# One store of the block inverses per half of the rows, and an instruction order from the timeline model, in a hybrid mLSTM and gated-delta-rule block

## The chip, the cores and the metric

The kernel runs on one core of one Trainium2 chip. The metric is the time of one execution on the device in microseconds (us). The changed kernel is compared with the kernel before on the same chip.

The core has five engines that this text names as the profile does: PE (TensorE, matmuls; PEld is its weight load), DVE (VectorE), ACT (ScalarE), POOL (GpSimd) and SP (SyncE). Each works through its own list of instructions strictly in order, and waits at an instruction until what it needs is there. DMAs are issued from the lists of SP, POOL and ACT.

## The reference

One encoder block over 256 tokens of 2048 features, in float32: an adaptive norm, one large input projection, two bidirectional mixers, a gated merge, an output projection, and a SwiGLU FFN.

```python
def gated_delta_chunkwise(q, k, v, beta, g):        # 16 heads of 128, CHUNK = 64
    ...
    a_mat = jnp.eye(CHUNK, dtype=jnp.float32) + (
        betac[..., :, None] * jnp.einsum('nbhid,nbhjd->nbhij', kc, kc) * decay_strict)
    t_mat = lax.linalg.triangular_solve(
        a_mat, jnp.broadcast_to(jnp.eye(CHUNK, dtype=jnp.float32), a_mat.shape),
        left_side=True, lower=True, unit_diagonal=True)
    ...
def mlstm_chunkwise(q, k, v, log_i, log_f):         # 4 heads, dk 256, dv 512
    ...
```

Branch A is the mLSTM, branch B the gated delta rule (GDN). The merge is `g_a*y_a + g_b*y_b`, where y_a and y_b are the branches after a projection each. The inverse `t_mat` is what the change touches.

## The kernel before, in words

All weights are read once from DRAM as f32 and split on the chip into a high part (`wh`, by ACT) and the remainder (`wl`, by DVE, which subtracts `wh` from the raw weights). PE multiplies with wh and wl. A weight tile is loaded by SP into one of three buffers `raw`; wh and wl have three buffers each.

The work comes in jobs. `fjob` (L157 to L163; names `b..` for the GDN's q, k, v and `a..` for those of the mLSTM) makes 128 columns out of two halves; a half is one wh on ACT, one wl on DVE and 24 matmuls of 256 columns, 16 on wh and 8 on wl. `tjob` (L182, L183, L200 to L203; names `z`, `v`, `o`, `ma`, `mb`, `ya`, `yb`, `gt`, `up`, `d`) makes 512 columns; each half has one wh, one wl and 12 matmuls of 512 columns, 8 on wh and 4 on wl. Jobs whose result is wanted only later are used to fill PE's time beside steps that need little PE (`fill` in the code, "fill jobs" below).

The stages in order of time: the first 130 us read the adaptive norm's weights and the first input weights; then to some 965 us the GDN, in four groups g0 to g3 of four heads, with fill jobs; the mLSTM with the output projections of both branches and the merge to about 1360 us; then the FFN to the end.

A group of the GDN has these steps:

- `gdn_phase1` for each head: convolution (`cv`, L298 to L301), norms, the decay-weighted Gram matrices `mi`. The 32x32 blocks on their diagonals go through DRAM (`inst_d`, L604) into the tile `uu` (L607), one block per partition, 64 blocks for the group.
- `gdn_invert`: DVE inverts the 64 blocks of 32x32 at once, from row 30 up to row 0, with one product (`utmp`, L635) and one addition (L641) a row. Rows 16 to 31 are stored to `inv_d` in DRAM after step 16, rows 0 to 15 at the end, by POOL (L627).
- `gdn_blocks`: POOL reads `inv_d` back into `cg` (L654), another layout of the same blocks. It takes the buffer of `uu`. DVE transposes it (L656) and mixes it into `R` (L660, L661); ACT copies it into `X` (L669) and `UL` (L674).
- `gdn_phase2` for each pair of heads: matmuls `p` (L689, L698, L723) on R, X and UL, then the recurrences, and at the end `px` (L772), `obt` (L774) and its store to `ob_d` (L775, issued from ACT).

After the last group the GDN's pools are closed (`sx.close()`), and the tiles of the mLSTM take their place. So POOL's loads for the mLSTM wait for the last uses of the GDN's tiles, the store of the last `obt` among them: `o` (L895, the GDN's result, split into `obh` and `obl`, L899 and L900, which the job `yb` multiplies), and for each head `mkq`, `vt`, `sgo` and `bc` (L904 to L911). `psc` (L924) multiplies mkq; `mdec` (L915 to L918, L933 to L936) is made from bc and psc; `pden` and `ph` use mdec.

The order of the instructions on each engine isn't the order of the code. The framework schedules the traced program on a model of the engines, and emits each engine's list in the order that comes out. Instructions that the code wraps in `order` (L85) keep the program's order among themselves:

```python
def order(ins, yes=True):
    return tc.keep_in_program_order(ins) if yes else ins
```

The model used is set where the context is made (L1361), `tile.TileContext(nc)`.

## Time and profile before

| | |
|---|---|
| median of 3 runs | 2038.97 us (2037.25 to 2042.45) |
| the profiled execution | 2036.88 us, its span 2035.0 us |
| mean granted TensorE clock | 0.987 |
| PE busy | 1956.7 us (96%) |
| DVE, ACT, POOL busy | 1394.1, 1050.0, 106.4 us |
| read from DRAM, written | 467.07 MB, 16.82 MB; 238 GB/s over the span |
| chain that ended last | PE 70%, DMA 11%, DVE 9%, ACT 6% |

The span runs from the first to the last instruction of the profiled execution; 1.88 us lie around it. A row of the timeline has the start, the duration, engine, line, operation, tiles (buffer numbers left out) and, in brackets, the idle time of the engine just before and what ended it. A row of the waits has the total, the number of times and the longest.

### The profile page before, as it was taken

The numbers are of one execution on the slowest core, as the hardware profiler recorded it, in microseconds if no ns is written. First come the engines' busy times: TensorE is split into PE (matmuls) and PEld (weight loads), VectorE is DVE, ScalarE is ACT, GpSimd is POOL, SyncE is SP. The second block draws the span as 40 slices with busy tenths as digits, with TensorE's granted clock in tenths as the row PEclk, the third lists the DMA queues.
The fourth block names the chain that finished last, engine by engine and source line by source line (L and its number), as shares of the span: only waits on it lengthen the run. The fifth ranks groups of instructions, "written<-read, shape, count | busy, mean of one in ns | idle before, by whom it ended". The sixth has DMA issues, their size and how long they took to land.

```text
span 2035.0 us, 27065 instructions
## 1 busy us (share of the span) xinstructions
PE 1956.7 (96%) x10374; PEld 1706.4 (84%) x10374; DVE 1394.1 (69%) x2059; ACT 1050.0 (52%) x1582; POOL 106.4 (5%) x205
## 2 busy tenths in 40 slices
PE   8999999999999899999899999999999999999997
PEld 6777879988888788988878788778888888888886
DVE  5778777777889588855677679866666665555554
ACT  3147547755775577565444444554444444444443
POOL 0002210010101010100200000000000000000000
PEclk9999999999999899999999999999999999999999
DMA  9986664556766465766987669656767666566563
GB/s 399 420 325 222 178 215 153 190 171 220 241 230 197 178 211 212 243 238 240 360 297 264 212 245 390 256 186 249 252 244 262 235 246 212 204 206 204 199 200 142
DMA packets 78962, 485.64 MB, mean 239 GB/s; under 512 B 10585, under 2 KB 15969, under 8 KB 24433
## 3 DMA queue, kind: packets, MB, share of 16 engines
q1 hardware_dynamic: 63360, 450.95, 61.2%
q0 software_dynamic: 8160, 17.88, 3.8%
q10 hardware_dynamic: 7314, 15.10, 2.0%
q8 instruction: 81, 1.33, 0.3%
q14 instruction: 47, 0.39, 0.1%
HBM read 467.07 MB, written 16.82 MB: 238 GB/s over the span
## 4 chain that ended last, share of the span: by engine, by line
PE 70%; DMA 11%; DVE 9%; ACT 6%; issue 2%; POOL 1%; ACTq 0%; SPq 0%; DVEq 0%; POOLq 0%
PE acc_up L200 4%; PE acc_up L203 4%; PE acc_up L201 4%; PE acc_d L201 4%; PE acc_d L200 4%; PE acc_d L203 4%; PE acc_gt L201 4%; PE acc_gt L200 4%; PE acc_gt L203 4%; PE acc_b L161 3%; DMA ra<-ada 3%; DMA ada<-ada 2%; PE acc_o L203 2%; PE acc_o L200 2%; PE acc_o L201 2%
## 5 line engine op out<-in xcount | busy, mean ns | idle before, releaser
L183 DVE TENSOR_TENSOR wl_d<-raw_d,wh_d 128x1024 fp32r<-128x1024 f32 x88 | 107.5, 1225 | 105.4 <-ACT wh_d L182 103.1
L183 DVE TENSOR_TENSOR wl_up<-raw_up,wh_up 128x1024 fp32r<-128x1024 f32 x88 | 107.6, 1225 | 100.4 <-ACT wh_up L182 100.4
L126 DVE SCALAR_TENSOR_TENSOR ada<-ada,crow 128x2048 f32<-128x2048 f32 x64 | 146.6, 2290 | 24.1 <-DMA ada<-ada 24.0
L182 ACT ACTIVATE wh_d<-raw_d 128x1024 fp32r<-128x1024 f32 x88 | 92.9, 1056 | 124.5 <-PE acc_d L201 114.3
L183 DVE TENSOR_TENSOR wl_gt<-raw_gt,wh_gt 128x1024 fp32r<-128x1024 f32 x88 | 107.7, 1224 | 69.9 <-ACT wh_gt L182 68.4
L182 ACT ACTIVATE wh_up<-raw_up 128x1024 fp32r<-128x1024 f32 x88 | 92.9, 1057 | 120.9 <-PE acc_up L201 71.6
L161 PE MATMUL acc_b<-hh,wh_b 128*128 128x256 f32 x576 | 142.0, 288 | 9.6 <-ACT wh_b L157 8.0
L182 ACT ACTIVATE wh_gt<-raw_gt 128x1024 fp32r<-128x1024 f32 x88 | 92.9, 1055 | 108.9 <-PE acc_gt L201 61.3
L161 PE MATMUL acc_b<-hl,wh_b 128*128 128x256 f32 x576 | 139.6, 284 | 0.0
L201 PE MATMUL acc_gt<-wh_gt,hfl 128*128 128x512 f32 x352 | 136.9, 389 | 0.0
L200 PE MATMUL acc_gt<-wh_gt,hfh 128*128 128x512 f32 x352 | 135.6, 385 | 0.0
L200 PE MATMUL acc_up<-wh_up,hfh 128*128 128x512 f32 x352 | 133.4, 379 | 0.0
L201 PE MATMUL acc_up<-wh_up,hfl 128*128 128x512 f32 x352 | 133.4, 379 | 0.0
L200 PE MATMUL acc_d<-wh_d,ffh 128*128 128x512 f32 x344 | 130.8, 380 | 0.0
L201 PE MATMUL acc_d<-wh_d,ffl 128*128 128x512 f32 x344 | 130.5, 379 | 0.0
L161 PEld LDWEIGHTS acc_b<-hh,wh_b 128*128 128x128 f32 x576 | 114.6, 199 | 10.2 <-ACT wh_b L157 8.5
L511 PE MATMUL first<-x,raw 128*128 128x256 f32 x512 | 114.5, 382 | 6.6 <-ACT x L504 6.6
L511 PEld LDWEIGHTS first<-x,raw 128*128 128x128 f32 x512 | 96.0, 190 | 25.1 <-ACT x L504 12.6
L161 PEld LDWEIGHTS acc_b<-hl,wh_b 128*128 128x128 f32 x576 | 114.8, 199 | 0.0
L300 DVE SCALAR_TENSOR_TENSOR cv<-pad,pk,cv 128x256 f32<-128x256 f32 x192 | 90.8, 481 | 20.2 <-ACT cv L298 18.2
L158 DVE TENSOR_TENSOR wl_b<-raw_b,wh_b 128x1024 fp32r<-128x1024 f32 x72 | 86.9, 1220 | 23.7 <-ACT wh_b L157 20.6
L182 ACT ACTIVATE wh_o<-raw_o 128x1024 fp32r<-128x1024 f32 x64 | 67.4, 1056 | 60.1 <-PE acc_o L201 27.2
(369 smaller groups left out, 5016.4 us busy)
## 6 DMA issues: line engine op xcount, KB each, us to landing
ada<-ada SPq DMA_DIRECT2D x64, 1024.0 KB, 5.2
raw_gt<-wgu SPq DMA_DIRECT2D x44, 1024.0 KB, 5.0
raw_up<-wgu SPq DMA_DIRECT2D x44, 1024.0 KB, 4.9
raw_d<-wd SPq DMA_DIRECT2D x44, 1024.0 KB, 4.9
raw_b<-winb SPq DMA_DIRECT2D x36, 1024.0 KB, 5.1
ra<-ada SPq DMA_DIRECT2D x32, 1025.0 KB, 15.7
raw<-win SPq DMA_DIRECT2D x16, 1024.0 KB, 14.5
raw_z<-wint SPq DMA_DIRECT2D x16, 1024.0 KB, 5.1
```

What stands on the lines that cost most here:

```text
L126: V.scalar_tensor_tensor(raw, raw, 1.0, row_c[:, :D], ALU.mult, ALU.mult, accum_out=mod[:, c0 + b : c0 + b + 1])
L158: V.tensor_tensor(wl, raw[:, k0 : k0 + 8], wh.bitcast(F32), ALU.subtract)
L161: PE.matmul(o, wh[:, k], both(x, k0 + k).rearrange("p a b -> p b a"), start=k0 + k + i == 0, stop=False)
L182: order(S.activation(wh, raws[u][:, k0 : k0 + 2], AF.Copy), early)
L183: order(V.tensor_tensor(wl, raws[u][:, k0 : k0 + 2], wh.bitcast(F32), ALU.subtract), early)
L200: order(PE.matmul(ps[t], tok(xh, kk, t), turns(wh[:, k]), start=kk == 0, stop=False), early and steps > 1)
L201: PE.matmul(ps[t], tok(xl, kk, t), turns(wh[:, k]), start=False, stop=False)
L203: PE.matmul(ps[t], tok(xh, kk, t), turns(wl[:, k]), start=False, stop=kk == last)
L300: V.scalar_tensor_tensor(cv, pd[:, i : i + T], w[i], cv, ALU.mult, ALU.add)
L511: PE.matmul(first[o], raw[:, o], x[:, b], start=b == 0 and o % 2 == 0, stop=b == KB - 1 and o % 2 == 1)
```

## The change

It has two parts.

**The store of the inverses.** `inv_d` gets the layout row j, block p, column i, in place of j, block row, and head within it. The blocks of head `hl_` now go to every fourth partition of `uu` (from `hl_` on), not to sixteen in a row. With that the 64 partitions stand in the order in which `cg` wants them, and a half of the rows is stored by one DMA of 64 x 16 x 32 instead of four of 16 x 16 x 32. POOL's list has 24 DMAs fewer for it (32 become 8 over the four groups). The number of bytes and of 128-byte pieces stays, as do the loads of `cg`, four a group.

**The order.** The context is made with `schedule_with_timeline_sim=True`: the lists of all engines come from the framework's timeline model instead of its plain one. Of PE's 9627 instructions 3831 stand at another place, of DVE's 1348 and of ACT's 1439; SP's list is nearly as before. The instructions are the same, except that ACT loads its function tables 57 times, not 68.

```diff
-    inv_d = [tc.dram_tile([32, 4, 16, 32], F32, name=f"inv_d{g}") for g in range(NH_B // GRP)]
+    inv_d = [tc.dram_tile([32, 64, 32], F32, name=f"inv_d{g}") for g in range(NH_B // GRP)]
...
-        G.dma_start(uus[g][16 * hl_ : 16 * hl_ + 16], inst)
+        G.dma_start(uus[g][hl_::GRP], inst)
...
-        inv = inv_d[g].rearrange("j b (x h) i -> h (b x) j i", h=GRP)
 
         def store(rows):
-            for e in range(GRP):
-                G.dma_start(inv[e, :, rows], uu[16 * e : 16 * e + 16, rows])
+            G.dma_start(inv_d[g][rows].rearrange("j p i -> p j i"), uu[:, rows])
...
         for b in range(4):
-            G.dma_start(cg[32 * b : 32 * b + 32, 0], inv_d[g][:, b].rearrange("j x i -> j (x i)"))
+            G.dma_start(cg[32 * b : 32 * b + 32, 0], inv_d[g][:, 16 * b : 16 * b + 16].rearrange("j m i -> j (m i)"))
...
-    with tile.TileContext(nc) as tc:
+    with tile.TileContext(nc, schedule_with_timeline_sim=True) as tc:
```

Lines behind the store stand two lines earlier after the change (L656 becomes L654, L774 becomes L772).

The end of the inversion of group 2 on DVE, before. The names are those above; `wl_ma_1_0` is the wl of the fill job ma, tile 1, first half.

```order
860 L183 TENSOR_TENSOR wl_ma_1_0_5970<-raw_ma_1_5967,wh_ma_1_0_5969 128x1024
861 L635 TENSOR_TENSOR utmp_5529<-uu_4526 64x30
862 L641 TENSOR_TENSOR uu_4526<-uu_4526,utmp_5529 64x30
863 L183 TENSOR_TENSOR wl_ma_1_2_5986<-raw_ma_1_5967,wh_ma_1_2_5985 128x1024
864 L183 TENSOR_TENSOR wl_ma_2_0_6004<-raw_ma_2_6001,wh_ma_2_0_6003 128x1024
865 L183 TENSOR_TENSOR wl_ma_2_2_6020<-raw_ma_2_6001,wh_ma_2_2_6019 128x1024
866 L183 TENSOR_TENSOR wl_ma_3_0_6038<-raw_ma_3_6035,wh_ma_3_0_6037 128x1024
867 L183 TENSOR_TENSOR wl_ma_3_2_6054<-raw_ma_3_6035,wh_ma_3_2_6053 128x1024
868 L656 STREAM_TRANSPOSE cg_5926<-cg_5926 128x512
```

The same place on DVE, after; `wl_b` belongs to the GDN's own fjob for a later head.

```order
868 L183 TENSOR_TENSOR wl_mb_0_0_6065<-raw_mb_0_6062,wh_mb_0_0_6064 128x1024
869 L633 TENSOR_TENSOR utmp_5517<-uu_4514 64x30
870 L639 TENSOR_TENSOR uu_4514<-uu_4514,utmp_5517 64x30
871 L158 TENSOR_TENSOR wl_b_0_0_6095<-raw_b_0_6092,wh_b_0_0_6094 128x1024
872 L126 SCALAR_TENSOR_TENSOR ada_8_6165,mod<-ada_8_6165,crow 128x2048
873 L158 TENSOR_TENSOR wl_b_0_8_6138<-raw_b_0_6092,wh_b_0_8_6137 128x1024
874 L158 TENSOR_TENSOR wl_b_1_0_6185<-raw_b_1_6182,wh_b_1_0_6184 128x1024
875 L158 TENSOR_TENSOR wl_b_1_8_6228<-raw_b_1_6182,wh_b_1_8_6227 128x1024
876 L300 SCALAR_TENSOR_TENSOR cv_0_6174<-pad_134,pk,cv_0_6174 128x256 x3
877 L654 STREAM_TRANSPOSE cg_5908<-cg_5908 128x512
```

The last addition (L641, then L639) has moved behind the splits of the job ma, and the splits of four halves of an fjob and three convolution steps stand between it and the transpose.

The end of the GDN on ACT, before: the last `obt` (L774) and what follows it.

```order
909 L774 ACTIVATE obt_8863<-px_1_8741,pk 128x256
910 L321 DMA kq_d_97<-ev_a_0_8858 128x256
911 L775 DMA ob_d_117<-obt_8863 128x256
912 L774 ACTIVATE obt_8868<-px_1_8741,pk 128x256
913 L157 ACTIVATE wh_a_1_8_8920<-raw_a_1_8890 128x1024
914 L775 DMA ob_d_117<-obt_8868 128x256
915 L157 ACTIVATE wh_a_2_0_8972<-raw_a_2_8970 128x1024
916 L157 ACTIVATE wh_a_2_8_9000<-raw_a_2_8970 128x1024
917 L157 ACTIVATE wh_a_3_0_9034<-raw_a_3_9032 128x1024
```

The same place on ACT, after.

```order
895 L772 ACTIVATE obt_8839<-px_1_8717,pk 128x256
896 L773 DMA ob_d_117<-obt_8839 128x256
897 L182 ACTIVATE wh_ma_3_2_9227<-raw_ma_3_9209 128x1024
898 L182 ACTIVATE wh_yb_0_0_9270<-raw_yb_0_9268 128x1024
899 L772 ACTIVATE obt_8844<-px_1_8717,pk 128x256
900 L773 DMA ob_d_117<-obt_8844 128x256
901 L182 ACTIVATE wh_yb_0_2_9286<-raw_yb_0_9268 128x1024
902 L182 ACTIVATE wh_yb_1_0_9339<-raw_yb_1_9337 128x1024
```

The last `obt` stood among the halves of the job a (with the rest of a and the job ma behind it), and now stands behind nearly all of both, next to the first halves of yb. On PE it is the same: between the last px and the first matmul of yb stand 27 matmuls of the job ma now.

## The prediction

> **What bounds the kernel now.** I read the page's busy times and its chain first, then the busy times in 40 us windows, and then the waits.

> ```profile
> PE 1956.7 (96%) x10374; PEld 1706.4 (84%) x10374; DVE 1394.1 (69%) x2059; ACT 1050.0 (52%) x1582; POOL 106.4 (5%) x205
> PE 70%; DMA 11%; DVE 9%; ACT 6%; issue 2%; POOL 1%; ACTq 0%; SPq 0%; DVEq 0%; POOLq 0%
> 280.00:320.00 40.00, 36.50 (x215) 33.61 (x213) 21.40 (x35) 21.28 (x36) 4.21 (x8) 0.91 0.52 181
> 680.00:720.00 40.00, 33.92 (x257) 33.44 (x257) 22.32 (x31) 25.34 (x51) 0.00 (x0) 0.85 0.55 196
> 960.00:1000.00 40.00, 34.39 (x238) 31.90 (x238) 20.83 (x27) 19.27 (x28) 10.56 (x17) 0.94 0.86 323
> 1400.00:1440.00 40.00, 40.00 (x190) 34.83 (x189) 23.97 (x24) 17.80 (x19) 0.00 (x0) 1.00 0.72 261
> ```

> TensorE is busy 96% of the span. The window columns are start:end and length, then busy time of PE, PEld, DVE, ACT and POOL, then granted clock, DMA share and GB/s. From 1400 us (the FFN) PE is full, at clock 1.00: no order makes that stage shorter while its matmuls stay. What a new order can win is in the windows that hold less than 40 or a clock under 1: the GDN stage and the entry of the mLSTM.

> Next I looked at who waits there: the waits, POOL, DVE and ACT around the inversion of group 2, and the PE rows that begin with idle time (in brackets: idle before, and what ended it), in the same order as the four groups.

> ```profile
> DVE cg L656 <- DMA cg<-inv_d: 28.4, 4, 8.6
> POOL cg L654 <- DMA inv_d<-uu: 22.0, 4, 7.3
> ```
> ```profile
> 657.87 2.22 POOL L627 DMA_DIRECT2D inv_d<-uu  x4 [13.10 <-DVE uu L641]
> 665.33 1.99 POOL L654 DMA_DIRECT2D cg<-inv_d  x4 [5.23 <-DMA inv_d<-uu]
> ```
> ```profile
> 657.40 0.18 DVE L641 TENSOR_TENSOR uu<-uu,utmp 64x30 f32<-64x30 f32 x1
> 672.11 0.71 DVE L656 STREAM_TRANSPOSE cg<-cg 128x512 f32<-128x512 f32 x1 [6.48 <-DMA cg<-inv_d]
> 663.31 1.06 ACT L182 ACTIVATE wh_ma<-raw_ma 128x1024 fp32r<-128x1024 f32 x1 [1.53 <-PE acc_ma L201]
> 665.90 1.06 ACT L182 ACTIVATE wh_mb<-raw_mb 128x1024 fp32r<-128x1024 f32 x1 [1.53 <-PE acc_ma L201]
> 672.85 1.71 ACT L669 ACTIVATE X<-cg 32x256 f32<-32x256 f32 x4 [5.90 <-DVE cg L656]
> ```
> ```profile
> 216.77 0.48 PE L203 MATMUL acc_v<-wl_v,hh 128*128 128x512 f32 x1 [1.99 <-DVE wl_v L183]
> 302.08 1.54 PE L203 MATMUL acc_o<-wl_o,hh 128*128 128x512 f32 x4 [3.50 <-DVE wl_o L183]
> 488.22 1.08 PE L689 MATMUL p<-R,cc 128*128 128x32 f32 x8 [2.57 <-DVE R L661]
> 675.03 1.13 PE L203 MATMUL acc_mb<-wl_mb,hh 128*128 128x512 f32 x4 [1.40 <-DVE wl_mb L183]
> 678.56 0.58 PE L161 MATMUL acc_b<-hh,wh_b 128*128 128x256 f32 x1 [1.59 <-ACT ev_ma L313]
> 693.70 0.58 PE L161 MATMUL acc_b<-hh,wh_b 128*128 128x256 f32 x1 [3.69 <-ACT wh_b L157]
> 708.51 0.38 PE L161 MATMUL acc_b<-hh,wh_b 128*128 128x256 f32 x1 [2.39 <-ACT wh_b L157]
> 873.79 1.05 PE L689 MATMUL p<-R,cc 128*128 128x32 f32 x8 [2.02 <-DVE R L661]
> ```

> So the inverse takes a round trip: last addition at 657.58, four stores, their landing, four loads, their landing, transpose at 672.11: 14.5 us. DVE stands before the transpose and ACT before X, in order, so neither splits weights for the fill jobs; PE runs dry shortly after. In group 2 it goes on, since ACT's late split also holds up the buffers of the next weights. After an idle time comes a stretch at clock 0.50:

> ```profile
> 217.30:224.10 6.80, 6.80 (x23) 5.71 (x22) 3.77 (x11) 2.92 (x9) 0.21 (x1) 0.50 0.80 175
> 302.80:309.40 6.60, 6.60 (x31) 6.42 (x31) 4.51 (x5) 3.27 (x4) 0.00 (x0) 0.50 0.37 117
> 678.20:681.50 3.30, 2.94 (x14) 2.94 (x15) 2.66 (x4) 0.79 (x2) 0.00 (x0) 0.50 0.52 149
> 691.90:698.50 6.60, 4.80 (x22) 4.80 (x23) 4.70 (x6) 5.32 (x7) 0.00 (x0) 0.50 0.37 127
> 709.00:712.20 3.20, 3.20 (x17) 3.20 (x16) 2.85 (x3) 2.33 (x5) 0.00 (x0) 0.50 0.26 38
> 995.70:1002.30 6.60, 4.70 (x11) 3.80 (x12) 5.32 (x11) 0.00 (x0) 1.93 (x3) 0.50 1.02 379
> ```

> Its price is half of PE's busy time in it.

> **Term 1, the stores.** Eight POOL issues of an inversion become two. Three fewer after the last addition are 3 x 0.555 = 1.7 us of POOL (2.22 for four), all on the round trip, if the one issue of 64 partitions is as short as one of 16; if it costs as four did, nothing. The landing of a 64-partition store isn't in the trace: the waits give 22.0 / 4 = 5.5 us after four, at most 7.3, and I take the same 5.5, with -2 and +4 as bounds. On the two middle stores (row 16) nothing waits. The load into every fourth partition moves the same blocks: nothing. The new round trip is then 12.8 us.

> **Term 2, the order around the inversions.** In the new order ACT and DVE split four or five more weight halves between the last addition and the transpose, or have the transpose later by as much; X moves the same way on ACT. A half of a tjob is worth 665.90 - 663.31 = 2.59 us of PE, and one of an fjob 2.70:

> ```profile
> 702.55 1.79 PE acc_b L161 x16
> 704.34 0.91 PE acc_b L163 x8
> ```

> In group 2 the rows behind the last addition hold four fjob halves, 10.8 us, and PE has the one or two halves ahead of them still to do (2.6 to 5.2): 13.4 to 16.0 us of matmuls against 12.8 of round trip. More than that, ACT's weights no longer stand behind X, so the raw buffers turn over and the tail of group 2 (1.59, 3.69, 2.39) loses its cause. What can go: group 0 3.50 + 6.60 / 2 = 6.8; group 1 2.6; group 2 1.40 + 1.59 + 3.69 + 2.39 = 9.1, and (2.94 + 4.80 + 3.20) / 2 = 5.5; group 3 2.0. Ahead of it the wait of 216.77 with its slow stretch, 1.99 + 3.4 = 5.4, since DVE now has convolution steps between the splits and not eight of them ahead of wl_v. Together 31.4. The cover of group 2 is close, and what is late next there is the wl_b behind the transpose; I leave 3.7 there, and half of the 5.4 as unproven. Gain: 25.

> **Term 3, the end of the GDN.** Less fill after the inversions' groups means that the last heads' steps stand behind it: the last px now has only three matmuls and 24 of the job ma3 between it and the first yb0, which needs o. Before, the rest of the jobs a and half of ma lay between that px and psc0 (964.63 to 990.38 below, 25.8 us). The mLSTM loads on POOL are behind the last store of obt in both.

> ```profile
> 964.63 0.38 PE L772 MATMUL px<-cst,on 128*128 128x128 f32 x2
> 968.31 1.57 POOL L895 DMA_DIRECT2D o<-ob_d  x2 [100.11 <-ACT wh_a L157]
> 977.61 1.06 ACT L899 ACTIVATE obh<-o 128x1024 fp32r<-128x1024 f32 x1
> 985.58 0.54 POOL L911 DMA_DIRECT2D bc<-mal_d  x1 [3.33 <-DMA mkq<-kq_d]
> 990.38 1.89 PE L924 MATMUL psc<-mkq 128*128 128x256 f32 x8
> 997.60 3.78 PE L924 MATMUL psc<-mkq 128*128 128x256 f32 x8 [5.33 <-DMA mkq<-kq_d]
> 1003.46 0.34 DVE L936 SCALAR_TENSOR_TENSOR mdec<-psc,eT,mdec 128x128 f32<-128x128 f32 x1
> ```

> Counted from the px at 964.63, obh is there after 14.0 us (978.67), mkq of head 0 after 20.9, of head 1 after 33.0, its decay after 39.2 (1003.80). A matmul of 512 columns takes 2.59 / 12 = 0.216, so PE is at yb0 after 27 x 0.216 = 5.8: it waits 8.2, and about 1 for obl; then 24 matmuls, psc0 (no wait), 28 matmuls, psc1 (4.2 wait), pden1 (about 4). Upper bound: 17.4 of waits and about 5 of half clock, 22.4, in place of 5.33 + 4.70 / 2 = 7.7: a loss of 14.7. Lower bound: the loads are quicker, because with PE standing no new weights are asked for, and in the new SP order two gate loads stand later; they shared 323 GB/s at a DMA share of 0.86 in that window. If half the bytes there were weights, the loads come in half the time: 7 for obh, 1 to 2 us of wait: a gain of 5. I take 12.7 of waits and slow clock, nearer the upper end since the first o comes behind weights already asked for: a loss of 5.

> **Term 4, the rest of the order.** The waits of PE from 130 to 1000 us that are not tied to the above begin with these two (total, times, longest):

> ```profile
> PE acc_z L200 <- ACT wh_z L182: 4.8, 3, 2.8
> PE vps L555 <- ACT vf L301: 3.2, 5, 1.4
> ```

> Ten further causes have 2.3 us and less each; I count some 20 us in all. A new order drops some and makes others. Bounds -8 and +8, taken at +3, because each fill half that now covers an inversion is missing at a smaller wait. ACT has eleven fewer table loads; ACT at 52% isn't the bound: nothing. In the FFN the order is the same: nothing.

> Sum against the profiled execution, 2036.88 us (span 2035.0, 1.88 around it): -25 + 5 + 3 = -17, so 2019.9. That execution lies 2.1 under the median of 2038.97, hence **2022**.

> **A rule weighed.** In the rows a slow stretch follows idle times of only 1.99 and 2.39 us. [...] The sum would be 5 less gain (half of 6.80 and of 3.20) and some 3 less loss, 2024, inside the forecast's range; chance 0.2. [...]

> **Rivals.**
> - *The entry of the mLSTM costs more than the inversions give: slower.* If the loads bind all four heads, heads 2 and 3 wait as head 1 does (4.2 + 4 each): 14.7 + 16.4 = 31 lost, and PE half-clocked in the 20.8 us of matmuls between: 10 more. 2036.9 - 25 + 41 + 2.1 = 2055. It decides once that place loses over 31. For it: obh at 14.0 against 5.8. Against: the loads' rate rises when PE stands. 0.13.
> - *The fill is only moved: same.* PE's work and the round trips are as long as before; waits saved at the inversions come back at smaller steps, p to px, which now have less between them: term 4 at +20 instead of 3: 2039. For it: about 20 us of small waits there already. Against: the fill at the inversions came from the end, where 25 us lay. 0.15.
> - *The single store is slow.* If it lands 4 us later and saves no issue, the round trip is 18.5, over the 16.0 of cover: groups 0 and 2 stand again for some 3 us and their slow stretches, about 12 back: 2034. For it: nothing shows 1024 pieces in one store; against: the four share the same queue. 0.10.
> - *All goes,* 31.4 and the entry's 7.7 as well: 2036.9 - 39 + 2.1 = 2000. 0.07.

> **How the numbers follow.** The forecast has 0.55, with 2010 to 2034 its own range (gain of 25 to 31, entry -5 to +15, rest 8 each way, not all at one end). A time within 0.3% (6 us, about what a measurement tells from no change) is 2033 to 2045. Faster: 0.53 + 0.05 of the slow store + 0.07 + 0.03 of the moved fill = 0.68. Same: 0.02 + 0.05 + 0.10 + 0.01 = 0.18. Slower: 0.12 + 0.02 = 0.14. The range 2005 to 2044 leaves out most of the first rival and of the last.

> **What would show it.** Right: the DVE row of the transpose idle under 2 us in all four groups, PE rows behind it without idle time, clock 1.00 from 280 to 320 and 680 to 720, one POOL issue of about 0.6 us a store; and a wait of 5 to 9 us at the first yb0, released by obh. Wrong: a store landing of over 8 us; p or px rows with new waits of 2 to 3 us; or waits at psc in heads 2 and 3 also, with a clock of 0.5 around.

## The result, and the profile after

| | before | after |
|---|---|---|
| median of 4 runs | 2038.11 us (2036.98 to 2042.45) | 2025.41 us (2022.18 to 2029.46) |
| ratio, 95% interval | 1 | 0.9935 (0.9912 to 0.9958) |
| profiled execution, span | 2036.88, 2035.0 us | 2026.32, 2024.5 us |

The kernel is 12.7 us faster; 2022 was forecast, 17 us under the median then known. A second timing of both gave 0.9942 (0.9922 to 0.9963).

The page after, its busy times and its chain, and then the busy times in windows (columns as in the prediction); the first of the windows is from before, the other four are from after:

```profile
PE 1948.6 (96%) x10374; PEld 1709.0 (84%) x10374; DVE 1386.4 (68%) x2059; ACT 1036.8 (51%) x1571; POOL 95.2 (5%) x181
PE 72%; DVE 11%; DMA 9%; ACT 5%; issue 3%; POOL 0%; SPq 0%; ACTq 0%; DVEq 0%; POOLq 0%
```
```profile
140.00:180.00 40.00, 35.62 (x163) 30.25 (x162) 37.73 (x69) 32.51 (x47) 4.22 (x7) 1.00 0.62 217
140.00:180.00 40.00, 31.70 (x135) 26.33 (x134) 33.98 (x66) 27.98 (x44) 4.17 (x7) 0.91 0.57 175
280.00:320.00 40.00, 40.00 (x279) 37.64 (x278) 31.96 (x60) 23.79 (x31) 2.83 (x5) 1.00 0.61 210
680.00:720.00 40.00, 38.22 (x293) 36.29 (x292) 34.16 (x60) 32.17 (x68) 0.87 (x2) 0.96 0.64 235
960.00:1000.00 40.00, 27.37 (x141) 23.46 (x140) 17.50 (x24) 18.94 (x32) 6.29 (x10) 0.85 0.75 262
```

The first inversion's window is full now (36.50 busy at clock 0.91 before), the third has 38.22 instead of 33.92. The entry of the mLSTM has lost 7 us (34.39 before), and the window of the z job nearly 4. The transposes of groups 0 and 2, and four PE rows that begin with a wait (at z, behind the inversions of groups 1 and 2, and at the first yb), after:

```profile
309.51 0.71 DVE L654 STREAM_TRANSPOSE cg<-cg 128x512 f32<-128x512 f32 x1 [0.52 <-DMA cg<-inv_d]
679.24 0.70 DVE L654 STREAM_TRANSPOSE cg<-cg 128x512 f32<-128x512 f32 x1
```
```profile
157.50 0.80 PE L203 MATMUL acc_z<-wl_z,hh 128*128 128x512 f32 x1 [7.17 <-DVE wl_z L183]
493.56 0.63 PE L687 MATMUL p<-R,cc 128*128 128x32 f32 x4 [1.65 <-DVE R L659]
689.87 0.38 PE L161 MATMUL acc_b<-hh,wh_b 128*128 128x256 f32 x1 [1.63 <-ACT wh_b L157]
997.70 0.79 PE L200 MATMUL acc_yb<-wh_yb,obh 128*128 128x512 f32 x1 [12.59 <-ACT obh L897]
```

DVE comes to these transposes with 0.52 and no idle time, where it stood 8.62 and 6.48; in groups 1 and 3 it stands 1.83 and nothing, 6.32 and 6.99 before. PE's two longest waits from 130 to 1000 us are new: 7.17 at a wl_z, and 12.59 at the first yb.

To see where time went in all kernels I took from the trace, for every matmul, the time from its start to the next one's start, less the 20th percentile of that spacing for the same tiles and shape over the twelve profiles; summed by stage this is PE's lost time (waits and slow clock together), in us. "Inversions" is 270 to 360, 470 to 530, 640 to 725 and 860 to 925 us, "between" the rest of 360 to 860. Two profiles of the changed kernel differ by up to 3 in a stage: smaller differences say nothing. A profile is one execution only: that of the store alone is the fastest of its six (2022.34, median 2026.35), and that of store and 10 halves the slowest of its six (2033.44, median 2028.07).

| kernel (ratio to before) | z and v jobs, 140-270 | inversions | between | end of GDN, entry, 925-1060 | 1060-1360 | all, with the rest |
|---|---|---|---|---|---|---|
| before | 11.1 | 37.7 | 19.6 | 11.0 | 27.5 | 132.4 |
| after (0.9935) | 12.1 | 15.5 | 23.4 | 19.9 | 26.3 | 121.0 |
| after, again (0.9942) | 11.7 | 12.4 | 24.5 | 18.3 | 25.4 | 115.4 |
| store alone (0.9948) | 10.6 | 30.1 | 18.0 | 9.1 | 25.5 | 118.0 |
| order alone (0.9954) | 12.1 | 17.2 | 24.1 | 16.5 | 26.7 | 120.1 |
| 12 halves, plain order (0.9960) | 11.0 | 15.5 | 21.2 | 23.5 | 27.4 | 123.8 |
| store and 10 halves (0.9952) | 10.2 | 17.6 | 22.2 | 21.6 | 31.3 | 128.8 |

The inversions gained 22 to 25 us; 7 to 9 were given back at the end of the GDN, and 4 to 5 between the inversions.

### The profile page after: what moved, and what is told of

Same layout as the page of the kernel before. It is cut to its first block, busy times and chain, and to the rows that moved or that the text cites. A ratio compares the mean times of both kernels' runs of the same rounds, so it can differ in the third digit from the quotient of the medians.

```text
span 2024.5 us, 27066 instructions
## 1 busy us (share of the span) xinstructions
PE 1948.6 (96%) x10374; PEld 1709.0 (84%) x10374; DVE 1386.4 (68%) x2059; ACT 1036.8 (51%) x1571; POOL 95.2 (5%) x181
## 4 chain that ended last, share of the span: by engine, by line
PE 72%; DVE 11%; DMA 9%; ACT 5%; issue 3%; POOL 0%; SPq 0%; ACTq 0%; DVEq 0%; POOLq 0%
PE acc_up L201 4%; PE acc_up L203 4%; PE acc_up L200 4%; PE acc_d L200 4%; PE acc_d L201 4%; PE acc_d L203 4%; PE acc_gt L200 4%; PE acc_gt L201 4%; PE acc_gt L203 4%; DMA ra<-ada 3%; PE acc_a L161 2%; PE acc_o L203 2%; PE acc_o L200 2%; PE acc_o L201 2%; PE acc_b L161 2%
## 5 line engine op out<-in xcount | busy, mean ns | idle before, releaser
L183 DVE TENSOR_TENSOR wl_d<-raw_d,wh_d 128x1024 fp32r<-128x1024 f32 x88 | 107.7, 1224 | 102.3 <-ACT wh_d L182 100.3
L183 DVE TENSOR_TENSOR wl_up<-raw_up,wh_up 128x1024 fp32r<-128x1024 f32 x88 | 107.6, 1225 | 99.3 <-ACT wh_up L182 99.3
L182 ACT ACTIVATE wh_d<-raw_d 128x1024 fp32r<-128x1024 f32 x88 | 92.9, 1056 | 128.5 <-PE acc_d L201 122.9
L182 ACT ACTIVATE wh_gt<-raw_gt 128x1024 fp32r<-128x1024 f32 x88 | 92.9, 1056 | 120.7 <-PE acc_gt L201 73.2
L182 ACT ACTIVATE wh_up<-raw_up 128x1024 fp32r<-128x1024 f32 x88 | 93.0, 1056 | 119.2 <-PE acc_up L201 72.5
L183 DVE TENSOR_TENSOR wl_gt<-raw_gt,wh_gt 128x1024 fp32r<-128x1024 f32 x88 | 107.0, 1224 | 67.5 <-ACT wh_gt L182 46.7
L161 PE MATMUL acc_b<-hh,wh_b 128*128 128x256 f32 x576 | 140.0, 285 | 5.5 <-ACT wh_b L157 5.5
L161 PE MATMUL acc_b<-hl,wh_b 128*128 128x256 f32 x576 | 137.6, 281 | 0.0
L200 PE MATMUL acc_gt<-wh_gt,hfh 128*128 128x512 f32 x352 | 136.0, 386 | 0.0
L201 PE MATMUL acc_gt<-wh_gt,hfl 128*128 128x512 f32 x352 | 135.2, 384 | 0.0
L200 PE MATMUL acc_up<-wh_up,hfh 128*128 128x512 f32 x352 | 133.4, 379 | 0.0
L201 PE MATMUL acc_up<-wh_up,hfl 128*128 128x512 f32 x352 | 133.4, 379 | 0.0
L200 PE MATMUL acc_d<-wh_d,ffh 128*128 128x512 f32 x344 | 130.8, 380 | 0.0
L201 PE MATMUL acc_d<-wh_d,ffl 128*128 128x512 f32 x344 | 130.8, 380 | 0.0
L161 PEld LDWEIGHTS acc_b<-hh,wh_b 128*128 128x128 f32 x576 | 111.7, 194 | 8.5 <-ACT wh_b L157 6.6
L161 PEld LDWEIGHTS acc_b<-hl,wh_b 128*128 128x128 f32 x576 | 111.7, 194 | 1.8 <-issue 1.7
L157 ACT ACTIVATE wh_b<-raw_b 128x1024 fp32r<-128x1024 f32 x72 | 75.3, 1056 | 55.8 <-DMA raw_b<-winb 29.3
L182 ACT ACTIVATE wh_o<-raw_o 128x1024 fp32r<-128x1024 f32 x64 | 67.4, 1057 | 66.1 <-PE acc_o L201 30.7
## 6 DMA issues: line engine op xcount, KB each, us to landing
ra<-ada SPq DMA_DIRECT2D x32, 1025.0 KB, 15.7
raw<-win SPq DMA_DIRECT2D x16, 1024.0 KB, 14.5
```

What stands on the lines that cost most here:

```text
L157: S.activation(wh, raw[:, k0 : k0 + 8], AF.Copy)
L161: PE.matmul(o, wh[:, k], both(x, k0 + k).rearrange("p a b -> p b a"), start=k0 + k + i == 0, stop=False)
L182: order(S.activation(wh, raws[u][:, k0 : k0 + 2], AF.Copy), early)
L183: order(V.tensor_tensor(wl, raws[u][:, k0 : k0 + 2], wh.bitcast(F32), ALU.subtract), early)
L200: order(PE.matmul(ps[t], tok(xh, kk, t), turns(wh[:, k]), start=kk == 0, stop=False), early and steps > 1)
L201: PE.matmul(ps[t], tok(xl, kk, t), turns(wh[:, k]), start=False, stop=False)
```

## The experiments

Each ratio is to the kernel before, run beside it on the same chip.

**The two parts alone, and both once more.** `store_only` has all edits of the change but the last line, and so the plain model; `order_only` has only the last line.

```diff
-    with tile.TileContext(nc, schedule_with_timeline_sim=True) as tc:
+    with tile.TileContext(nc) as tc:
```

> The single store and its layout, with the plain model's order (DVE, ACT and PE lists as before but for a few neighbours). Theory A (the order is what gains, the store shortens a round trip that is still uncovered): the round trip goes from 13.5-15.9 us to 11-14, each of the four PE waits behind it gets about 2 us shorter (3.50, 2.57, 1.40 and its tail, 2.02), so 4 to 10 us: 2028 to 2034. Theory B (the store is the whole change): about 2025, as with both. Theory C (the store is worth nothing on the chip): 2037 to 2040, waits unchanged.

> The timeline model's order with the four stores of before; all lists but POOL's are those of the changed kernel. Theory A (the order covers the round trip, the store is then nearly redundant): 2024 to 2030; the transposes come 2 us later, groups 0 and 2 show no new PE wait, group 1's wait of 1.65 and group 3's transpose (idle 4.66) grow by 2 at most. Theory B (the store is the whole change): 2036 to 2045, with the waits of before back.

> The changed kernel itself, beside the others of this call. It should lie at 0.992 to 0.996 of the kernel before, as it did (0.9935); with the store alone at 0.9948 and the order alone at 0.9954 it tells whether the two parts add up (0.990) or cover the same waits (0.993 to 0.995).

Measured: store alone 2026.35 us, 0.9948 (0.9930 to 0.9966); order alone 2026.18 us, 0.9954 (0.9939 to 0.9969); both again 2025.57 us, 0.9942. If the parts added up, both would give 0.990; they don't. Each alone gives most of the gain: the order alone falls in the range of its theory A, and the store alone gains more than its theory A had (2028 to 2034) and comes to the number of its theory B. But the store isn't the whole change, as theory B has it, since the order gains as much without it. The intervals of the three overlap, so that both together are faster than either alone isn't shown. Waits in the store alone, and below them the store's group in the changed kernel (min/median/max ns of an issue):

```profile
DVE cg L654 <- DMA cg<-inv_d: 18.7, 4, 6.7
POOL cg L652 <- DMA inv_d<-uu: 15.6, 4, 6.0
```
```profile
L625 POOL DMA_DIRECT2D inv_d<-uu x8: 835/846/877, 277.2 to 851.2; - x8
```

The one store is issued in 0.84 us, not 0.56, so 1.4 us are saved of 2.22. In the store alone POOL waits 15.6 / 4 = 3.9 us for its landing instead of 5.5. With the loads of cg that followed, the round trips (last addition to last landing of cg) were 11.2, 10.1, 10.4 and 13.0 us, 15.9, 13.5, 14.4 and 15.7 before. The waits of DVE fall from 28.4 to 18.7, and the stage's lost time by 7.6; nothing is given back at the end, where the store alone loses 9.1. The order alone (PE and POOL waits):

```profile
PE acc_yb L200 <- ACT obh L899: 12.2, 1, 12.2
PE p L689 <- DVE R L661: 3.2, 1, 3.2
POOL cg L654 <- DMA inv_d<-uu: 15.6, 4, 5.5
```

It covers round trips of 10.1, 17.8, 13.6 and 11.5 us with matmuls: only group 1, with 17.8, shows a wait of 3.2. And it pays 12.2 at yb. So the store shortens the wait, the order covers it, and done together each finds little left of what the other would have saved.

One thing does not fit a store that lands sooner by itself. In the new order POOL waits 3.9 us for the four stores and 18.5 / 4 = 4.6 for the one, and the mean round trip is 13.3 with four stores and 12.8 with one (12.3 in its second profile), where the plain order has 14.9 and 11.2. Only the 1.4 us of issue are saved in both orders; why the landings differ from order to order stays open.

**Cover without the new order.** The kernel before, with four more halves of fill between the loads of cg and the transpose; and the store alone with two more.

```diff
-        fill(8)
+        fill(12)
```

> The kernel before (four stores, plain order), with 12 instead of 8 halves of the fill jobs traced between the loads of cg and the transpose: four more halves, 10.4 us of matmuls, in each round trip. Theory 'cover' (what the new order gains is that more splits stand ahead of the transpose): the waits of 3.50, 2.57, 1.40/1.59/3.69/2.39 and 2.02 and the slow stretches at 302 and 678 to 712 go, 10 to 20 us faster: 2017 to 2027. Theory 'conserved' (16 halves less fill elsewhere cost as much): 2033 to 2045, with new waits at the p to px steps and at the mLSTM loads.

> The single store in the plain order, with 10 instead of 8 halves of fill jobs in each round trip. With the store the round trip was 10.1 to 13.0 us and DVE still stood 3.0 to 6.7 us before the transposes; two halves are 5.2 us, so those waits should nearly go, while only 8 halves are taken from the end (16 with fill12). Theory (cover against entry): faster than the store alone (0.9948) and than fill12 (0.996): 0.990 to 0.993, 2018 to 2024. Rival (the end of the GDN gives all of it back): 0.994 to 0.997.

Measured: 12 halves 2028.78 us, 0.9960 (0.9944 to 0.9975); store and 10 halves 2028.07 us, 0.9952 (0.9933 to 0.9970). The first group's transpose, and the PE rows at the end of the GDN, with 12 halves; then the PE waits there with store and 10 halves:

```profile
300.89 0.71 DVE L656 STREAM_TRANSPOSE cg<-cg 128x512 f32<-128x512 f32 x1
```
```profile
984.89 0.69 PE L772 MATMUL px<-cst,on 128*128 128x128 f32 x2 [6.42 <-ACT obt L774]
997.54 0.80 PE L200 MATMUL acc_yb<-wh_yb,obh 128*128 128x512 f32 x1 [11.96 <-ACT obh L899]
```
```profile
PE psc L922 <- DMA raw_yb<-wbb: 5.7, 1, 5.7
PE psc L922 <- DMA mkq<-kq_d: 5.2, 1, 5.2
PE pb L745 <- DVE r L746: 3.7, 1, 3.7
```

With four stores and round trips of 13.2 to 16.9 us, DVE comes to the transposes with at most 0.97 us of idle time, and the inversions lose 15.5 us, as much as in the changed kernel. So cover (matmuls that PE has at hand during the round trip) is what removes those waits; the new order is one way to have it. But the fill is gone at the end: 6.42 at the last px and 11.96 at yb, 23.5 lost there instead of 11.0. The time, 2028.78, lies between the ranges of the two theories: the waits went, as the one said, and much of the gain came back, as the other did. With the store and 10 halves, 12.5 are won at the inversions against the store alone, and 12.5 lost at the end (the two profiles lie at opposite ends of their runs, as said above). The medians show no gain over the store alone, as the rival said. Nor did two more halves cover all: DVE still stood 2.45 and 4.37 us before the transposes of groups 1 and 2.

**The entry of the mLSTM.** `o_early` gives the o of the first group a tile on the other side of the memory, which does not wait for the last obt. `hold_ma3` keeps the last fill job out of the last group's fill and its 96 matmuls behind the last px.

```diff
-        o4 = ml.tile([P, 4, T], F32, tag="o4", bufs=2, name=f"o4_{g}")
+        o4 = (ml if g else ol).tile([P, 4, T], F32, tag="o4", bufs=2 if g else 1, name=f"o4_{g}")
```
```diff
+            with tc.issue_after(last_px[0]) if name == "ma3" else ExitStack():
                 ...
+        held = fills.pop() if g == 3 else None
         ...
     sx.close()
+    fills.append(held)
```

> The changed kernel, with the o of the first group loaded into a tile that does not wait for the last obt. Theory (the 12.6 us wait at yb0 is the load of o behind the last store of obt): yb0's first two halves (24 matmuls, 5.2 us) run at once, the wait moves to psc0 or the second o and falls to 5 to 8 us, half-clock stretch shorter: 4 to 7 us faster than the changed kernel. Rival (yb0 waits on something else, or the o load is still queued behind the rest on POOL): no difference over 2 us.

> The changed kernel, with the matmuls of the last fill job (ma3, 96 of 512 columns, 20.7 us) held on PE behind the last px. Theory 'conserved' (the chain of the last heads has a length of its own; the fill only changes sides): PE waits some 12 to 15 us before the last px instead of 12.6 at yb0: 2023 to 2030. Theory 'misplaced' (the fill's splits on DVE and ACT also delayed the chain): px comes 10 us or more earlier, the 12.6 and its half clock go, no new wait over 3 us ahead of px: 2010 to 2018.

Measured: `o_early` 2023.37 us, 0.9930 (0.9911 to 0.9948); `hold_ma3` 2020.66 us, 0.9922 (0.9903 to 0.9940). Both intervals overlap those of the changed kernel widely. PE rows of the first, then of the second:

```profile
991.69 0.79 PE L200 MATMUL acc_yb<-wh_yb,obh 128*128 128x512 f32 x1 [4.95 <-ACT obh L899]
1010.23 0.58 PE L948 MATMUL pden<-ones,mdec 128*128 128x1 f32 x2 [5.59 <-DVE mdec L933]
```
```profile
961.62 0.59 PE L773 MATMUL px<-cst,on 128*128 128x128 f32 x2 [3.17 <-DVE on L793]
963.96 0.66 PE L773 MATMUL px<-cst,on 128*128 128x128 f32 x2 [1.75 <-DVE on L793]
```

The 12.6 at yb was the load of o: with an early o for the first group, two halves of yb run and the wait is 4.95. But 5.59 come back at pden, which needs the later loads; the stage loses 21.2, not less. Against the changed kernel beside it (2025.57) the gain is 2.2 us, not the 4 to 7 expected. With the fill held back, the last px runs at 964 and not at 979. That is no proof that the fill's splits had held up that chain: 69 of the fill's matmuls stood ahead of the px, and 69 x 0.216 = 14.9 us of PE's time moved behind it. The wait at yb is gone, but there are waits at px (3.17 and 1.75) and of 2.5 at a wl of yb, and the stage loses 19.7. Of each theory half came: the px is earlier and the wait at yb goes, but the waits come back at px and yb, and what the stage loses stays. The time, 2020.66, lies between their ranges.

**The wait at z.** `z_first` keeps the convolution steps of heads 1 and 2 behind the seventh wl of z on DVE (tile 3, first half; the expectations call it the sixth).

```diff
+        with tc.issue_after(wls["z0", 3, 0].ins) if ps is None and h in (1, 2) else ExitStack():
             for i in (0, 1, 3, 4):
```

> The changed kernel, with the convolution steps of heads 1 and 2 (first batch) kept behind the sixth wl of z on DVE. Theory: the wait of 7.17 at 150 us and its half clock (3.4) come from eight convolution steps that the new order put ahead of wl_z; then the wait falls under 3 us, the slow stretch at 155 goes and the kernel is 5 to 9 us faster than the changed one: 2016 to 2021. Rival: ACT's table loads and wh_z are as late, the wait only changes its name: within 2 us of the changed kernel.

Measured: 2022.27 us, 0.9925 (0.9907 to 0.9944).

```profile
153.78 0.70 PE L205 MATMUL acc_z<-wl_z,hh 128*128 128x512 f32 x2 [3.30 <-DVE wl_z L185]
164.72 0.79 PE L202 MATMUL acc_z<-wh_z,hh 128*128 128x512 f32 x1 [4.63 <-ACT wh_z L184]
```

The 7.17 becomes 3.30, so the convolution steps caused about half of it. The splits still start 2.0 us later than before (152.51 against 150.54): DVE stands 2.54 us ahead of them, waiting for a tile `u` of ACT, and stood 0.25 there before. And 4.63 come up at wh_z, as the rival said (2.8 in the kernel before). The stage goes from 12.1 to 10.9, within its spread, and the time misses the theory's 2016 to 2021.

**Both edits together,** run twice.

> The changed kernel with both edits tried singly before: the last fill job behind the last px, and the convolution steps of heads 1 and 2 behind the sixth wl of z. Singly they gave 0.9922 and 0.9925 of the kernel before, against 0.9935 for the changed kernel. If their gains are real and independent, 0.990 to 0.992 (2016 to 2021); if they are within the spread, 0.993 to 0.995.

> The changed kernel with both edits again (the last fill job behind the last px; convolution steps of heads 1 and 2 behind the sixth wl of z), which gave 0.9910. If that holds: 0.989 to 0.993; if it was chance, 0.993 to 0.995 like the changed kernel.

Measured: 2019.14 us, 0.9910 (0.9891 to 0.9929), then 2022.33 us, 0.9936 (0.9920 to 0.9951). The first alone would have passed for a better kernel; the second is where the changed kernel lies. The end of the GDN lost 16.1 and 14.8 in their two profiles, 19.9 and 18.3 in those of the changed kernel. A version that beats the changed kernel in time is not shown.

## Why the prediction was right, point by point

- *Term 1, the store:* the round trip was put at 12.8 us; in the changed kernel the four were 10.3, 16.4, 11.7 and 12.8, in the mean 12.8. That is luck: the parts differ, with 1.4 us of issue saved, not 1.7, and a landing of 4.6, not 5.5, and the same order with four stores has 13.3, so that in this order the store is worth 0.5 to 1 us of round trip. What the term did not price is the store without the order: alone it is worth 10 us of time, since the shorter round trip (11.2 for 14.9 in the mean) takes time off each of the four uncovered waits.
- *Term 2, the cover:* 25 forecast, 22.3 of it at the inversions and 2.7 at the wait of 216.77. The inversions gave 22.2 and 25.3 in the two profiles. The second part failed: the wait of 216.77 went, but the z job ahead of it waits 7.17. The new order put seven more convolution steps ahead of three splits of z, and DVE waits 2.3 us for ACT there; the same row before and after, by which the splits start 5.7 us later:

```profile
150.54 3.49 DVE L183 TENSOR_TENSOR wl_z<-raw_z,wh_z 128x1024 fp32r<-128x1024 f32 x3
```
```profile
156.23 3.49 DVE L183 TENSOR_TENSOR wl_z<-raw_z,wh_z 128x1024 fp32r<-128x1024 f32 x3
```

  The stage went from 11.1 to 12.1 and 11.7 where a gain of 2.7 was counted. The loss of 1 us is within the spread, but the 2.7 did not come. The term priced the job v, and not the job z just ahead of it, where the wait is now.
- *Term 3, the entry:* a loss of 5 forecast between -5 and +14.7; it was 7 to 9 over the stage, so the term was too small by 2 to 4. Its shape was not as drawn: one wait of 12.59 at yb, above the 8.2 worked out as the most, and then none at psc. These PE and POOL rows show why:

```profile
978.90 0.38 PE L770 MATMUL px<-cst,on 128*128 128x128 f32 x2
985.70 1.57 POOL L893 DMA_DIRECT2D o<-ob_d  x2 [125.88 <-ACT wh_yb L182]
```

  The loads start 6.8 us after the last px and not 3.7 as before, mostly because the last obt's store landed in 4.4 us (1.7 before). The row names a split, wh_yb, as what ended the wait; but in five profiles of the new order (the changed kernel twice, `order_only`, `o_early` and `z_first`) the loads start 0.92 or 0.93 us after that store's landing. Two weight loads of yb, issued from 978.63 us on, run beside the store, issued at 980.33; whether they slow it was not tested. The first o then takes 10.8 us to land, 8.9 before. So obh is in use 18.8 us after px, where the prediction had it ready after 14.0. I took over the offsets of before, as if the store and the loads would land as fast beside the loads of yb. That loads come faster while PE stands was an estimate and is not shown: PE stood 12.59 us, and from 960 to 1000 us 262 GB/s were moved, 323 before.
- *Term 4, the rest:* +3 forecast. Between the inversions 4 to 5 were lost, and after 1060 us 3.0 and 4.5 won in the two profiles: the sum (about zero) is within 3 us of the forecast, its parts were not foreseen, and each is hardly clear of the spread.
- *The rivals:* "the fill is only moved" holds in part: half of what the inversions won is given back. It is also what decides in the experiments: where the store is already there, two more halves of cover win nothing. The slow store did not happen (it lands in 2.7 to 6.0 us), and neither did waits at psc, where the first rival had them for all four heads. No run shows the 5 less gain and the 3 less loss of the 2024 (chance 0.2): the slow stretches behind the waits of 1.99 and 2.39 us went with these waits. In the changed kernel the wait at wl_v is 0.7, those at wh_b are at most 1.6, and no stretch at clock 0.50 starts between 162 and 380 or between 695 and 936 us.
- *The signs named:* DVE's idle time under 2 us in all four groups came, and so did a wait at the first yb released by obh, but with 12.59 and not 5 to 9. The clock from 680 to 720 is 0.96 and not 1.00, a store is issued in 0.84 us and not 0.6, and PE rows behind the transposes still wait 1.65 (group 1) and 1.63 (group 2).
- *The sum:* -17 against the profiled execution; the two profiles after gave -10.6 and -15.9 of their own times, the medians -12.7. The forecast of the cover at the inversions held; the store's round trip came out by luck, and the losses elsewhere were put too low by some 4 us together (by the medians).

## What to carry to other kernels

A wait in a round trip through memory can be shortened or covered. Shortening it here (one DMA for four, in the plain order) gave 10 us and took nothing from elsewhere. Covering it by the order alone gave 20 us on the spot and gave back half: 5.5 at the end of the GDN, where the fill was missing and the next loads lay open, and 4.5 between the inversions. So before trusting an order that closes a gap, look for the place where that fill stood before, and price the loads there; and time such a result twice, since one and the same kernel here came to 0.9910 and then to 0.9936, which is 5 us.

## What the runs showed of the hardware

```profile
544.10:547.50 3.40, 1.97 (x17) 1.75 (x17) 2.97 (x16) 2.08 (x8) 0.00 (x0) 1.00 0.90 294
547.50:550.90 3.40, 3.33 (x30) 3.17 (x30) 3.40 (x11) 2.71 (x9) 1.10 (x2) 1.00 0.04 14
687.50:690.90 3.40, 1.77 (x16) 1.66 (x16) 2.02 (x3) 2.13 (x3) 0.00 (x0) 1.00 0.74 294
690.90:694.30 3.40, 3.40 (x19) 3.40 (x18) 3.29 (x7) 3.28 (x11) 0.00 (x0) 0.50 0.38 77
```

Behind the step with 1.97 us of work the clock was 1.00, behind the one with 1.77 us it was 0.50. Over the twelve profiles, from 15 us on, the step behind was slow in 94 of 94 cases with 2 us or more idle in a step, in 34 of 71 with 1.4 to 2.0, in 11 of 95 with 1.0 to 1.4, and in 25 of some 6700 with less (in the profiles before and after alone: 15 of 15, 8 of 16, 1 of 19 and 5 of 1121). Of these 25, 16 stand behind a step that was slow itself, and 9 behind a busy step at full clock, which idle time does not explain. By this count a wait of 1.6 us can cost 1.7 us more, or nothing (an estimate: half of a step of 3.41 us at clock 0.50); I take this, and where a wait falls on the grid, for a good part of the spread between runs of one kernel, which was not tested.
